# Low parts of the first projection's weights on VectorE, with the opening and the first feed-forward groups reordered

## The chip, the cores and the metric

The kernel runs on one core of one Trainium2 chip. The metric is the device time of one execution in microseconds; a kernel's time is the median of its runs. Five engines matter: TensorE (PE in the profile; its weight loads are PEld), VectorE (DVE), ScalarE (ACT), GpSimd (POOL), and SyncE (SP), which issues most DMAs.

## The reference

One block of a bidirectional encoder, on 1024 tokens of width 1024, in float32:

```python
h = layer_norm(x)
proj = h @ w_in                       # 1024 x 11776: q, k, v of 24 attention heads; q, two forget gates,
                                      # input and output gate of 8 recurrent heads; two merge gates
att = dilated_attention(aq, ak, av)   # three groups of 8 heads, dilations 1, 4, 16, windows of 128, 512, 2048
rec = hgrn2(hq, hf_fwd, hf_bwd, hi, hg, lower_bounds)   # chunkwise gated recurrence, both directions
merged = sigmoid(ga) * (att @ w_att_up) + sigmoid(gh) * (rec @ w_hgrn_up)
h = layer_norm(ALPHA * h + merged @ w_o)
gate, up = split(h @ w_ffn_in)        # 1024 x 5632
h = layer_norm(ALPHA * h + (silu(gate) * up) @ w_ffn_out)
```

## The kernel before

**Products in three passes.** Every float32 operand of a large product is split into a high part, `w_hi`, a cast to the rounded format that TensorE multiplies fast, and a low part, `w_lo = w - w_hi`. A product is `hi*hi + hi*lo + lo*hi`, three matmuls (`mm3`, L301 to L303), the third of which needs the low part of the weight:

```python
nc.tensor.matmul(ps, whi, xhi, start=first, stop=False, **kw)   # L301
nc.tensor.matmul(ps, whi, xlo, start=False, stop=False, **kw)   # L302
nc.tensor.matmul(ps, wlo, xhi, start=False, stop=last, **kw)    # L303
```

**Seven products for eight.** Each matrix product over 1024 x 256 of the weights and all tokens is done by a scheme of Strassen's kind: weights and activations are cut into 2 x 2 blocks, sums of blocks are made (`s1` to `s4` of the weights, `t1` to `t4` of the activations), and seven products of blocks, numbered 1, 2, 5, 6, 3, 7, 4 by `PRODUCTS`, take the place of eight. One product is twelve matmuls of 128 x 512 (four steps over the contraction, three passes), and its weight block, 128 x 4 x 128, is what the profile shows as 128x512. `wkeep` holds a partial result that was copied or added out of a PSUM bank; the last add goes into `evh`.

**The stream of the first projection (L556 to L658).** `stream` runs over groups of weight tiles, two groups (`g` = 0, 1) in turn. For each product `i` of the sequence it issues the sums of product `i + 5` (two on VectorE, L574 and L576 or L579, one on GpSimd, L575), then `prep(i + 3)`, then the twelve matmuls of product `i`, then its evacuation. `prep` makes the cast on ScalarE (`cast`, L585) and the low part (`rest`, L590) on GpSimd. Tiles `w_hi` and `w_lo` have four buffers each, so that weights are ready at most three products ahead. `evac_ahead` gives casts, lows and evacuations a higher priority than other work in the program's order.

**What runs between the products.** `phase1` puts pieces of other work between the steps of the stream: for the attention heads far and near units (`att_far`, `att_near`; the near unit scales its probabilities at L1159), and for each recurrent head `hgrn_side` with scans (L1263), reciprocals (L1274, L1277), products with them (L1278, L1279), and the chain of states `hR` (L1319, L1320), all on VectorE. At the end of the stream `load_split` (L1404) fetches the attention's output back and splits it, its low part (`att_lo`) on GpSimd, by L280.

**The opening (L661).** For the first two groups the order of work is written out by hand: the layer norm of the eight token blocks (`R.stats`, `R.norm`), transposes (`R.turn`), copies out of PSUM (`R.copy`), sums (`R.sum`), high and low parts of the activations (`R.hi`, L426, and `R.lo`, L432), and the first fourteen products, some in halves of 256 columns. Here the low parts of weights are on VectorE but for seven on GpSimd.

**The feed-forward opening (L1585 to L1627, and L1760 on).** `Group` does the same scheme for the feed-forward weights. The order around its first two groups, `g0` and `g1`, is again written out (`in_order`): `prep` makes a block's sum (L100), cast and low part (L276, L280), `late_block` fetches and splits one block of the activations as they arrive (`xb22`, `xt3`, `xt4`; four casts and four lows on VectorE), and `out` evacuates: a sum, a tanh on ScalarE (L1703) and a multiply on VectorE (L1704).

Each engine works through its own list of instructions; semaphores carry waits between engines. Weights come through DMAs that SyncE issues.

Of the kernel before, what the change touches and what calls it, by code (L numbers as in the profile page):

```python
# [81 lines left out]
class Group:  # L82
# [43 lines left out]
            o.nc.scalar.copy(t, ps)  # L126
        return t

    def out(self, i, l, ps, add):
        with self.o.tc.high_priority(offset=self.o.evac_ahead):  # L130
            self.evac(i, l, ps, add)

    def first(self):
        self.m1 = self.keep(self.product(1, 1, True))
# [15 lines left out]
class Block:  # L150
# [193 lines left out]
    def rows_in(self, pool):  # L344
# [14 lines left out]
        class Rows:  # L359
# [24 lines left out]
            @staticmethod  # L384
            def copy(t, q, on):
                g, b = self.col["gin"], self.col["bin"]
                if t < 4:
                    v = V[t, q] = self.half3("v11") if q == 0 else (
                        self.half3("v21") if t == 0 else pool.tile([128, 4, 128], F32, name=f"v21{t}"))
                else:  # L390
                    if q == 0:
# [164 lines left out]
    def stream(self, tiles):  # L556
# [37 lines left out]
        def prep(i):  # L594
            if i >= len(seq):
                return
            with tc.high_priority(offset=self.evac_ahead):
                cast(i)
                rest(i, nc.gpsimd)

        def bank(n, g, b):
            return self.ps_pj(2 * g + (n + b) % 2)
# [58 lines left out]
    def opening(self, pool, A, at, first, cast, rest, sums, product, evacuate):  # L661
# [63 lines left out]
        R.hi("b11", 2)  # L725
        R.hi("b21", 2)
        R.lo("b11", 2)
        R.turn(4, 0, 1)
        weight(2, 0, gps)
        R.copy(3, 0, "act")  # L730
        R.copy(3, 1, "dve")
        R.lo("b21", 2)
        R.norm(5)
        R.hi("b11", 3)
        R.hi("b21", 3)
        R.stats(6)
        R.lo("b11", 3)
        R.lo("b21", 3)
        weight(2, 1, gps)
        product(at[0, 2], 0)  # L740
        product(at[0, 1], 1)
        product(at[1, 1], 1)
# [4 lines left out]
        R.sum("t1", 4)  # L747
        R.hi("t1", 4)
        R.copy(4, 1, "act")
        R.lo("t1", 4)  # L750
# [5 lines left out]
        R.stats(7)  # L756
        R.copy(5, 0, "act")
        R.turn(6, 0, 1)
        sums(at[0, 6], dve)
        R.lo("t2", 4)  # L760
        evacuate(at[1, 1])
        R.sum("t1", 5)
        R.hi("t1", 5)
        R.copy(5, 1, "act")
        R.lo("t1", 5)
        cast(at[0, 6])
        R.sum("t2", 5)
        R.hi("t2", 5)
        R.norm(7)
        rest(at[0, 6], dve)  # L770
        R.copy(6, 0, "dve")
        sums(at[1, 6], dve)
        R.lo("t2", 5)
        cast(at[1, 6])
        evacuate(at[0, 2], later)
        cast(at[0, 5])
        product(at[0, 6], 0)
        R.turn(7, 0, 1)
        R.copy(6, 1, "act")
        evacuate(at[1, 2], later)  # L780
        R.sum("t1", 6)
        R.hi("t1", 6)
        rest(at[1, 6], dve)
        rest(at[0, 5], dve)
        R.copy(7, 0, "act")
        cast(at[1, 5])
        R.sum("t2", 6)
        R.hi("t2", 6)
        R.lo("t1", 6)
        rest(at[1, 5], dve)  # L790
        product(at[1, 6], 0)
        product(at[0, 5], 0)
        product(at[1, 5], 0)
        R.copy(7, 1, "act")
        R.sum("t1", 7)
        R.hi("t1", 7)
        R.lo("t2", 6)
        R.sum("t2", 7)
        R.hi("t2", 7)
        R.lo("t1", 7)  # L800
# [17 lines left out]
        evacuate(at[1, 6])  # L818
        R.sum("t3", 4)
        R.sum("t3", 5)  # L820
        R.hi("t3", 4, 5)
        evacuate(at[0, 5])
        R.sum("t3", 6)
        R.sum("t3", 7)
        evacuate(at[1, 5])
        R.lo("t3", 4, 5)
        R.hi("t3", 6, 7)
        R.lo("t3", 6, 7)
# [572 lines left out]
    def pool(self, name, side="left"):  # L1401
        return self.tc.tile_pool(name=name, bufs=1, side=side, reuse_waits="tile")

    def load_split(self, pool, src, hi, lo):  # L1404
        raw = pool.tile([128, T], F32, name="st_raw", tag="st", bufs=4)
        self.nc.sync.dma_start(raw, src)
        self.split(hi, lo, raw)

    def phase1(self):

# [17 lines left out]
        for k in work:  # L1428
# [16 lines left out]
            elif not units and not now:  # L1445
# [26 lines left out]
    def phase2(self):  # L1472
        nc = self.nc
        gc, bc = self.col["g1"], self.col["b1"]
        with ExitStack() as es:
# [208 lines left out]
    def ffn_in(self):  # L1684

        nc = self.nc
        with ExitStack() as es:
# [7 lines left out]
            def evac_of(f):  # L1695
                C[f] = c = fp.tile([128, T], F32, name="fc", tag="fc", bufs=4)
                th = fp.tile([128, T], F32, name="fth", tag="fth", bufs=2)

                def evac(i, l, ps, add):
                    s = slice(HALF * l, HALF * (l + 1))  # L1700
                    if i == 0:
                        nc.vector.tensor_add(c[:, s], add, ps)
                        nc.scalar.activation(th[:, s], c[:, s], AF.Tanh, scale=0.5)  # L1703
                        nc.vector.scalar_tensor_tensor(th[:, s], th[:, s], 1.0, c[:, s], op0=OP.add, op1=OP.mult)  # L1704
                        return
                    u = ps
                    if add is not None:
# [51 lines left out]
            for g, e in zip(self.ahead, self.first_evac):  # L1759
                g.evac = e  # L1760
            with self.in_order():
                g0.out(0, 0, g0.c11, g0.m1)
                g0.m5 = g0.keep(g0.product(5, 2, True))
                g1.prep(5)
                g0.u2 = g0.keep(g0.product(6, 1, False))
                g1.out(0, 0, g1.c11, g1.m1)
                g1.prep(6)
                splits = late_block(0)
                g0.prep(3)
                g1.m5 = g1.keep(g1.product(5, 2, True))  # L1770
# [7 lines left out]
                g0.out(0, 1, g0.product(3, 2, False), g0.u2)  # L1778
                g1.prep(3)
                splits = late_block(2)  # L1780
                g0.out(1, 1, g0.product(7, 1, False), g0.m5)
                g1.prep(7)
                g1.out(0, 1, g1.product(3, 2, False), g1.u2)
                g0.prep(4)
                for f in splits:
                    f()
                nxt = self.ffn_raws(FS[2])
                g1.out(1, 1, g1.product(7, 1, False), g1.m5)
                g0.out(1, 0, g0.product(4, 1, False), None)
            combine(0, 0)  # L1790
            held = (g1.out(1, 0, g1.product(4, 1, False), None) for _ in range(1))
# [350 lines left out]
```

## Time and profile before

| what | value |
| --- | --- |
| time, median of 3 runs (lowest, highest) | 2131.01 us (2128.5, 2132.04) |
| the profiled execution: its time, its span | 2132.19 us, 2130.4 us |
| mean granted TensorE clock | 0.984 |
| TensorE busy | 2040.0 us, 96% |
| VectorE busy | 1380.2 us, 65% |
| GpSimd busy | 1178.6 us, 55% |
| ScalarE busy | 918.1 us, 43% |

The span runs from the first to the last instruction. In a list of groups a row has line, engine, operation, tiles, shapes and count, then busy time in us, the mean of one in ns, and the idle time ahead of them with what ended it. A row of a timeline has start and length in us and, in brackets, the idle time just before with its releaser. A row of waits reads: who waited, for whom, total us, times, longest. A row of windows has the window, its length, the busy time of each engine asked for (PE, PEld, DVE, ACT, POOL in this order where all are shown), the granted clock, the DMA share and GB/s.

### The profile page before, as it was taken

The numbers are of one execution on the slowest core, as the hardware profiler recorded it, in microseconds if no ns is written. First come the engines' busy times: TensorE is split into PE (matmuls) and PEld (weight loads), VectorE is DVE, ScalarE is ACT, GpSimd is POOL, SyncE is SP. The second block draws the span as 40 slices with busy tenths as digits, with TensorE's granted clock in tenths as the row PEclk, the third lists the DMA queues.
The fourth block names the chain that finished last, engine by engine and source line by source line (L and its number), as shares of the span: only waits on it lengthen the run. The fifth ranks groups of instructions, "written<-read, shape, count | busy, mean of one in ns | idle before, by whom it ended". The sixth has DMA issues, their size and how long they took to land.

```text
span 2130.4 us, 31395 instructions
## 1 busy us (share of the span) xinstructions
PE 2040.0 (96%) x11037; PEld 1687.0 (79%) x11037; DVE 1380.2 (65%) x2176; ACT 918.1 (43%) x1871; POOL 1178.6 (55%) x943
## 2 busy tenths in 40 slices
PE   5899999999999999989999999999899999999998
PEld 5778887878878888778888788887688888888886
DVE  7857646876468754778535812347768778677965
ACT  6544454444544445544355432144444444444330
POOL 2366653566435764466644864342566777665553
PEclk9999999999999999999999999999999999999999
DMA  5443442435323453333433865333544544449685
GB/s 202 129 124 126 140 130 85 144 119 161 120 94 131 144 164 116 109 123 119 153 126 129 270 210 159 99 124 107 186 137 154 174 156 163 146 155 332 199 260 171
DMA packets 296448, 324.21 MB, mean 152 GB/s; under 512 B 15905, under 2 KB 212834, under 8 KB 296290
## 3 DMA queue, kind: packets, MB, share of 16 engines
q1 hardware_dynamic: 290272, 302.05, 44.1%
q10 hardware_dynamic: 6018, 20.16, 2.4%
q8 instruction: 87, 1.43, 0.3%
q14 instruction: 71, 0.58, 0.1%
HBM read 211.78 MB, written 110.36 MB: 151 GB/s over the span
## 4 chain that ended last, share of the span: by engine, by line
PE 61%; DVE 6%; issue 4%; POOL 4%; DMA 2%; ACT 1%; SPq 0%; DVEq 0%; POOLq 0%; ACTq 0%
PE pj L301 13%; PE pj L303 12%; PE pj L302 12%; PE sd L303 6%; PE sd L301 6%; PE sd L302 6%; POOL w_lo L590 2%; PE sd L1359 1%; ACT p L1137 1%; DMA wa<-in_w_in_dram 1%; DVE hR L1320 1%; PE sd L1173 1%; DVE p L1159 1%; POOL w_lo L280 1%; DVE hR L1319 0%
## 5 line engine op out<-in xcount | busy, mean ns | idle before, releaser
L590 POOL TENSOR_TENSOR w_lo<-wa,w_hi 128x512 fp32r<-128x512 f32 x268 | 376.3, 1413 | 256.5 <-ACT w_hi L585 248.3
L585 ACT CAST w_hi<-wa 128x512 fp32r<-128x512 f32 x276 | 169.8, 617 | 216.6 <-PE pj L302 149.8
L280 POOL TENSOR_TENSOR w_lo<-f_raw,w_hi 128x512 fp32r<-128x512 f32 x110 | 176.4, 1614 | 112.0 <-ACT w_hi L276 51.9
L303 PE MATMUL pj<-xb22hi,w_lo 128*128 128x512 f32 x268 | 107.2, 400 | 7.2 <-POOL w_lo L590 6.3
L301 PE MATMUL pj<-xb22hi,w_hi 128*128 128x512 f32 x268 | 107.8, 402 | 3.7 <-ACT wkeep L606 3.7
L301 PE MATMUL pj<-xt1hi,w_hi 128*128 128x512 f32 (+1 forms) x276 | 108.0, 391 | 3.2 <-DVE evh L475 2.1
L302 PE MATMUL pj<-xb22lo,w_hi 128*128 128x512 f32 x268 | 107.0, 399 | 0.7 <-DVE xb22lo L280 0.7
L303 PE MATMUL pj<-xt1hi,w_lo 128*128 128x512 f32 (+1 forms) x276 | 106.6, 386 | 0.7 <-POOL w_lo L280 0.7
L302 PE MATMUL pj<-xt1lo,w_hi 128*128 128x512 f32 (+1 forms) x276 | 106.7, 387 | 0.0
L276 ACT CAST w_hi<-f_raw 128x512 fp32r<-128x512 f32 x110 | 67.8, 619 | 82.7 <-DVE f_raw L100 29.2
L575 POOL TENSOR_TENSOR wa<-wa,wa 128x512 f32<-128x512 f32 x44 | 62.0, 1410 | 72.2 <-DVE ws L574 58.7
L280 POOL TENSOR_TENSOR w_lo<-Wb,w_hi 128x512 fp32r<-128x512 f32 x47 | 64.5, 1374 | 58.2 <-ACT w_hi L276 56.7
L590 POOL TENSOR_TENSOR w_lo<-ws,w_hi 128x512 fp32r<-128x512 f32 x44 | 61.6, 1404 | 59.8 <-ACT w_hi L585 57.7
L301 PE MATMUL pj<-xb11hi,w_hi 128*128 128x512 f32 (+1 forms) x196 | 78.9, 403 | 6.4 <-DVE wkeep L507 4.0
L606 ACT COPY wkeep<-pj 128x512 f32<-128x512 f32 x138 | 80.2, 582 | 11.4 <-DVE evh L475 5.9
L301 PE MATMUL pj<-xt2hi,w_hi 128*128 128x512 f32 (+1 forms) x196 | 77.8, 397 | 5.3 <-ACT xt2hi L426 3.7
L574 DVE TENSOR_TENSOR ws<-wa,wa 128x512 f32<-128x512 f32 x46 | 39.5, 861 | 65.9 <-DMA wa<-in_w_in_dram 49.7
L303 PE MATMUL pj<-xt2hi,w_lo 128*128 128x512 f32 (+1 forms) x196 | 76.7, 391 | 5.5 <-POOL w_lo L590 5.3
L280 POOL TENSOR_TENSOR w_lo<-wsum,w_hi 128x512 fp32r<-128x512 f32 x44 | 66.0, 1499 | 28.1 <-ACT w_hi L276 27.5
L302 PE MATMUL pj<-xt2lo,w_hi 128*128 128x512 f32 (+1 forms) x196 | 76.8, 392 | 3.7 <-DVE xt2lo L432 3.7
L1311 ACT ACTIVATE hS<-hR,dec 128x128 f32<-128x128 f32 x112 | 44.5, 402 | 82.4 <-DVE hR L1320 59.1
L303 PE MATMUL pj<-xb11hi,w_lo 128*128 128x512 f32 (+1 forms) x196 | 77.7, 397 | 0.6 <-POOL w_lo L590 0.6
(431 smaller groups left out, 6620.5 us busy)
## 6 DMA issues: line engine op xcount, KB each, us to landing
wa<-in_w_in_dram SPq DMA_DIRECT2D x184, 256.0 KB, 3.1
f_raw<-in_w_ffn_in_dram SPq DMA_DIRECT2D x44, 512.0 KB, 4.2
Wb<-in_w_ffn_out_dram SPq DMA_DIRECT2D x40, 256.0 KB, 5.1
tg<-evh SPq DMA_DIRECT2D x32, 256.0 KB, 3.4
tg<-tg SPq DMA_DIRECT2D x16, 512.0 KB, 3.4
y<-ahs SPq DMA_DIRECT2D x16, 512.0 KB, 3.4
ah<-xt SPq DMA_DIRECT2D x8, 512.0 KB, 6.1
rec<-hg ACTq DMA_DIRECT2D x8, 512.0 KB, 3.5
```

Source lines behind the costliest of these rows:

```text
L276: nc.scalar.copy(hi, src)
L280: e.tensor_sub(lo, src, hi.bitcast(F32))
L301: nc.tensor.matmul(ps, whi, xhi, start=first, stop=False, **kw)
L302: nc.tensor.matmul(ps, whi, xlo, start=False, stop=False, **kw)
L303: nc.tensor.matmul(ps, wlo, xhi, start=False, stop=last, **kw)
L574: nc.vector.tensor_add(a["s1"], a["a21"], a["a22"])
L575: third.tensor_sub(a["a21"], a["a11"], a["a21"])
L585: nc.scalar.copy(ready[i][0], A[g][self.PRODUCTS[p][0]])
L590: e.tensor_sub(lo, A[g][self.PRODUCTS[p][0]], hi.bitcast(F32))
L606: nc.scalar.copy(t, ps)
L1137: nc.scalar.activation(z, z, AF.Exp, bias=N0[p, hd, tt:tt + 1], scale=QSCALE, accum_out=L0[p, hd, tt:tt + 1])
L1311: nc.scalar.activation(S[:, c, :], E, AF.Copy, scale=dec[:, 1, c:c + 1])
```

## The change

Four parts:

1. `prep` in `stream` calls `rest(i, nc.vector)`: the lows of the first projection's weights go from GpSimd to VectorE. In the instruction lists GpSimd has 5 of them in place of 312, VectorE 317 in place of 10.
2. `load_split` takes `parts`: the four low parts of the attention's output are made in two halves each, on VectorE.
3. In the opening some steps are put in another order, and two weights' lows go from GpSimd to VectorE.
4. In the feed-forward opening `g0.prep(5)` stands before the last turn and `g1.prep(5)` before the rest of it; the sums `s3` are named early, products are in another order, the splits of the late blocks come after the next weights' sums, and the multiply after the tanh (`bend`) is issued later than its tanh.

Three places show how the engines' lists change. The first is VectorE at the first recurrent head: `w_lo` is a low part of weights, `fa` and `fb` are the forget gates of the two directions, `qd` takes the reciprocals. Before:

```order
L579 TENSOR_TENSOR wa_943<-wa_943,wa_806 128x512
L1263 SCALAR_TENSOR_TENSOR fa<-fa,d_1123 128x512
L1274 RECIPROCAL qd<-fa 128x4x64 x2
L1263 SCALAR_TENSOR_TENSOR fa<-fa,d_1123 128x512
L1263 SCALAR_TENSOR_TENSOR fb<-fb,d_1126 128x528 x2
L507 TENSOR_TENSOR wkeep<-wkeep,pj 128x512
L1274 RECIPROCAL qd<-fa 128x4x64 x2
L1277 RECIPROCAL qd<-fb 128x4x64 x4
L486 TENSOR_TENSOR evh<-wkeep,pj 128x512
```

After:

```order
L590 TENSOR_TENSOR w_lo<-wa_765,w_hi 128x512
L1265 SCALAR_TENSOR_TENSOR fa<-fa,d_1123 128x512
L1265 SCALAR_TENSOR_TENSOR fb<-fb,d_1126 128x528
L1276 RECIPROCAL qd<-fa 128x4x64 x2
L1265 SCALAR_TENSOR_TENSOR fa<-fa,d_1123 128x512
L1279 RECIPROCAL qd<-fb 128x4x64 x2
L1265 SCALAR_TENSOR_TENSOR fb<-fb,d_1126 128x528
L590 TENSOR_TENSOR w_lo<-wa_815,w_hi 128x512
L507 TENSOR_TENSOR wkeep<-wkeep,pj 128x512
L590 TENSOR_TENSOR w_lo<-ws_1137,w_hi 128x512
L1276 RECIPROCAL qd<-fa 128x4x64 x2
```

The lows of two neighbouring products (`wa_765`, `wa_815`) now have four scans and four reciprocals between them, and the next low stands behind `wkeep`. (Line numbers behind the opening are shifted by the change: L1263 before is L1265 after, L1274 is L1276, L1277 is L1279.)

The second place is ScalarE in the opening, where a wait of TensorE ends: `wkeep` is a copy that frees a bank, `xt3hi` the high part of an operand. Before:

```order
L585 CAST w_hi<-wa_368 128x512
L606 COPY wkeep<-pj 128x512
L426 CAST xt3hi<-vt 128x4x128 x2
L606 COPY wkeep<-pj 128x512 x2
L426 CAST xt3hi<-vt 128x4x128 x2
```

After:

```order
L585 CAST w_hi<-wa_368 128x512
L606 COPY wkeep<-pj 128x512 x2
L426 CAST xt3hi<-vt 128x4x128 x2
L606 COPY wkeep<-pj 128x512
L426 CAST xt3hi<-vt 128x4x128 x2
```

One of the two copies behind the first pair of casts has moved ahead of it.

The third is VectorE in the feed-forward opening: `f_raw<-f_raw,wsum` is a sum of weights, `xb22lo` and `xt3lo` are low parts of late blocks of the activations, `fc` and `fth` an evacuation and its multiply (L1702 and L1704 before are L1709 and L1713 after). Before:

```order
L100 TENSOR_TENSOR f_raw<-f_raw,wsum 128x512
L280 TENSOR_TENSOR xb22lo<-t_raw,xb22hi 128x512 x4
L280 TENSOR_TENSOR xt3lo<-t_raw,xt3hi 128x512 x4
L1702 TENSOR_TENSOR fc<-wkeep,pj 128x512
L1704 SCALAR_TENSOR_TENSOR fth<-fth,fc 128x512
L100 TENSOR_TENSOR f_raw<-f_raw,wsum 128x512
```

After:

```order
L100 TENSOR_TENSOR f_raw<-f_raw,wsum 128x512
L1713 SCALAR_TENSOR_TENSOR fth<-fth,fc 128x512
L280 TENSOR_TENSOR xb22lo<-t_raw,xb22hi 128x512 x4
L1709 TENSOR_TENSOR fc<-wkeep,pj 128x512
L100 TENSOR_TENSOR f_raw<-f_raw,wsum 128x512
L1713 SCALAR_TENSOR_TENSOR fth<-fth,fc 128x512
L1709 TENSOR_TENSOR fc<-wkeep,pj 128x512
L280 TENSOR_TENSOR xt3lo<-t_raw,xt3hi 128x512 x4
```

The second sum has moved from behind both sets of four lows to between them.

The diff, cut to its core:

```diff
@@ -596,7 +596,7 @@
             with tc.high_priority(offset=self.evac_ahead):
                 cast(i)
-                rest(i, nc.gpsimd)
+                rest(i, nc.vector)
...
@@ -725,18 +725,20 @@
         R.lo("b11", 2)
+        R.norm(5)
         R.turn(4, 0, 1)
-        weight(2, 0, gps)
+        cast(at[0, 2])
         R.copy(3, 0, "act")
         R.copy(3, 1, "dve")
         R.lo("b21", 2)
-        R.norm(5)
+        rest(at[0, 2], dve)
...
         R.lo("b11", 3)
+        cast(at[1, 2])
         R.lo("b21", 3)
-        weight(2, 1, gps)
+        rest(at[1, 2], dve)
         product(at[0, 2], 0)
...
@@ -818,11 +820,11 @@
         evacuate(at[1, 6])
         R.sum("t3", 4)
         R.sum("t3", 5)
+        evacuate(at[0, 5])
         R.hi("t3", 4, 5)
-        evacuate(at[0, 5])
+        evacuate(at[1, 5])
         R.sum("t3", 6)
         R.sum("t3", 7)
-        evacuate(at[1, 5])
         R.lo("t3", 4, 5)
...
-    def load_split(self, pool, src, hi, lo):
+    def load_split(self, pool, src, hi, lo, parts=()):
         raw = pool.tile([128, T], F32, name="st_raw", tag="st", bufs=4)
         self.nc.sync.dma_start(raw, src)
-        self.split(hi, lo, raw)
+        if not parts:
+            self.split(hi, lo, raw)
+        for s in parts:
+            self.split(hi[:, s], lo[:, s], raw[:, s], eng_lo="dve")
...
-                    self.load_split(self.sp, self.att_d[i], self.ah[:, i, :], self.al[:, i, :])
+                    self.load_split(self.sp, self.att_d[i], self.ah[:, i, :], self.al[:, i, :],
+                                    [slice(0, HALF), slice(HALF, T)])
...
                 g0.first()
+                g0.prep(5)
                 second, last = turn(7)
-                g0.prep(5)
+                g0.prep(6)
                 second()
                 g1.first()
-                g0.prep(6)
+                g1.prep(5)
                 rest()
                 last()
...
             with self.in_order():
-                g0.out(0, 0, g0.c11, g0.m1)
+                bends = []
                 g0.m5 = g0.keep(g0.product(5, 2, True))
-                g1.prep(5)
-                g0.u2 = g0.keep(g0.product(6, 1, False))
-                g1.out(0, 0, g1.c11, g1.m1)
                 g1.prep(6)
                 splits = late_block(0)
+                g0.out(0, 0, g0.c11, g0.m1, bends)
+                g0.u2 = g0.keep(g0.product(6, 1, False))
                 g0.prep(3)
+                bends.pop()()
                 g1.m5 = g1.keep(g1.product(5, 2, True))
-                splits += late_block(1)
-                for f in splits[:4]:
+                for f in splits:
                     f()
+                splits = late_block(1)
+                g1.out(0, 0, g1.c11, g1.m1, bends)
+                g1.prep(3)
                 g1.u2 = g1.keep(g1.product(6, 1, False))
+                g0.sum("s3")
+                bends.pop()()
+                g0.out(0, 1, g0.product(3, 2, False), g0.u2, bends)
+                for f in splits:
+                    f()
                 g0.prep(7)
-                for f in splits[4:]:
+                splits = late_block(2)
+                g1.sum("s3")
+                bends.pop()()
+                g1.out(0, 1, g1.product(3, 2, False), g1.u2, bends)
...
```

More of the change, by code (lines that the diff above doesn't have):

```diff
@@ L127, in keep, with out @@
         return t
-    def out(self, i, l, ps, add):
+    def out(self, i, l, ps, add, later=None):
         with self.o.tc.high_priority(offset=self.o.evac_ahead):
-            self.evac(i, l, ps, add)
+            self.evac(i, l, ps, add, later)
     def first(self):
@@ L390, in copy @@
                 else:
-                    if q == 0:
+                    if (t, 0) not in V:
                         V[t, 0], V[t, 1] = hold("vt")[1]
@@ L749, in opening @@
         R.copy(4, 1, "act")
+        R.stats(7)
         R.lo("t1", 4)
@@ L755, in opening @@
         R.hi("t2", 4)
-        R.stats(7)
         R.copy(5, 0, "act")
         R.turn(6, 0, 1)
-        sums(at[0, 6], dve)
+        R.norm(7)
         R.lo("t2", 4)
@@ L764, in opening @@
         R.copy(5, 1, "act")
+        sums(at[0, 6], dve)
+        R.turn(7, 0, 1)
         R.lo("t1", 5)
@@ L768, in opening @@
         R.hi("t2", 5)
-        R.norm(7)
         rest(at[0, 6], dve)
+        R.copy(6, 1, "act")
+        R.lo("t2", 5)
         R.copy(6, 0, "dve")
[L772 to L780, printed above, removed]
         R.sum("t1", 6)
         R.hi("t1", 6)
[L783 to L786, printed above, removed]
+        product(at[0, 6], 0)
+        sums(at[1, 6], dve)
+        cast(at[1, 6])
         R.sum("t2", 6)
@@ L789, in opening @@
         R.lo("t1", 6)
+        evacuate(at[0, 2], later)
+        cast(at[0, 5])
+        R.copy(7, 0, "act")
+        R.lo("t2", 6)
+        evacuate(at[1, 2], later)
+        rest(at[1, 6], dve)
+        rest(at[0, 5], dve)
+        cast(at[1, 5])
+        R.copy(7, 1, "act")
+        R.sum("t1", 7)
+        R.hi("t1", 7)
         rest(at[1, 5], dve)
@@ L793, in opening @@
         product(at[1, 5], 0)
[L794 to L797, printed above, removed]
         R.sum("t2", 7)
@@ L1697, in evac_of, with evac @@
                 th = fp.tile([128, T], F32, name="fth", tag="fth", bufs=2)
-                def evac(i, l, ps, add):
+                def evac(i, l, ps, add, later=None):
                     s = slice(HALF * l, HALF * (l + 1))
@@ L1703, in evac, with bend @@
                         nc.scalar.activation(th[:, s], c[:, s], AF.Tanh, scale=0.5)
-                        nc.vector.scalar_tensor_tensor(th[:, s], th[:, s], 1.0, c[:, s], op0=OP.add, op1=OP.mult)
+                        def bend():
+                            nc.vector.scalar_tensor_tensor(th[:, s], th[:, s], 1.0, c[:, s], op0=OP.add, op1=OP.mult)
+                        if later is None:
+                            bend()
+                        else:
+                            later.append(bend)
                         return
@@ L1761, in ffn_in @@
             with self.in_order():
-                g0.out(0, 0, g0.c11, g0.m1)
+                bends = []
                 g0.m5 = g0.keep(g0.product(5, 2, True))
-                g1.prep(5)
-                g0.u2 = g0.keep(g0.product(6, 1, False))
-                g1.out(0, 0, g1.c11, g1.m1)
                 g1.prep(6)
                 splits = late_block(0)
+                g0.out(0, 0, g0.c11, g0.m1, bends)
+                g0.u2 = g0.keep(g0.product(6, 1, False))
                 g0.prep(3)
+                bends.pop()()
                 g1.m5 = g1.keep(g1.product(5, 2, True))
-                splits += late_block(1)
-                for f in splits[:4]:
-                    f()
+                for f in splits:
+                    f()
+                splits = late_block(1)
+                g1.out(0, 0, g1.c11, g1.m1, bends)
+                g1.prep(3)
                 g1.u2 = g1.keep(g1.product(6, 1, False))
-                g0.prep(7)
-                for f in splits[4:]:
-                    f()
-                g0.out(0, 1, g0.product(3, 2, False), g0.u2)
-                g1.prep(3)
-                splits = late_block(2)
+                g0.sum("s3")
[3 more added lines that the diff above has]
+                    f()
+                g0.prep(7)
+                splits = late_block(2)
+                g1.sum("s3")
+                bends.pop()()
+                g1.out(0, 1, g1.product(3, 2, False), g1.u2, bends)
+                g1.prep(7)
+                for f in splits[:2]:
+                    f()
+                bends.pop()()
                 g0.out(1, 1, g0.product(7, 1, False), g0.m5)
-                g1.prep(7)
-                g1.out(0, 1, g1.product(3, 2, False), g1.u2)
                 g0.prep(4)
-                for f in splits:
+                for f in splits[2:]:
                     f()
@@ L1788, in ffn_in @@
                 g1.out(1, 1, g1.product(7, 1, False), g1.m5)
+                g1.prep(4)
                 g0.out(1, 0, g0.product(4, 1, False), None)
```

## The prediction

> **What bounds the kernel now.** I read the page's span and busy times first, then who waits for whom, then single stretches.
>
> ```profile
> span 2130.4 us, 31395 instructions
> PE 2040.0 (96%) x11037; PEld 1687.0 (79%) x11037; DVE 1380.2 (65%) x2176; ACT 918.1 (43%) x1871; POOL 1178.6 (55%) x943
> ```
>
> TensorE sets the time: it is busy 2040.0 of 2130.4 us, so all that a change to other engines can win is about 90 us of idle TensorE, plus what idling costs in clock. The change adds and removes no matmul. The idle time has these owners (waits of TensorE, then of VectorE):
>
> ```profile
> PE pj L303 <- POOL w_lo L590: 12.4, 11, 2.7
> PE sd L1173 <- DVE p L1159: 8.4, 6, 2.7
> PE pj L301 <- DVE evh L475: 5.4, 5, 2.8
> PE sd L1336 <- DVE hR L1319: 4.8, 2, 4.2
> PE pj L301 <- DVE wkeep L507: 4.0, 1, 4.0
> ...
> DVE ws L574 <- DMA wa<-in_w_in_dram: 49.7, 21, 6.5
> ```
>
> A short stall can cost twice. The columns here are window, TensorE busy, granted clock, DMA:
>
> ```profile
> 459.50:463.00 3.50, 3.50 (x10) 0.51 0.23 80
> 1193.40:1200.20 6.80, 6.09 (x14) 0.50 0.93 315
> ...
> 458.40 0.47 PE L301 MATMUL pj<-xb11hi,w_hi 128*128 128x512 f32 x1 [3.96 <-DVE wkeep L507]
> 1194.11 0.79 PE L303 MATMUL pj<-xb22hi,w_lo 128*128 128x512 f32 x1 [2.62 <-POOL w_lo L590]
> 116.09 0.50 PE L303 MATMUL pj<-xb22hi,w_lo 128*128 128x512 f32 x1 [2.73 <-POOL w_lo L590]
> ...
> 116.00:123.00 7.00, 6.91 (x30) 5.74 (x31) 6.62 (x15) 4.39 (x10) 2.00 (x3) 1.00 0.60 189
> ```
>
> After the stall of 3.96 us the clock was 0.51 for 3.5 us: some 1.7 us of work lost. After the one of 2.62 it was 0.50 for 6.8 us: 3.4 lost. After the one of 2.73 at 116 us it stayed 1.00 (the column before the last two). So a stall of two to four us costs nothing, 1.7 or 3.4 us on top; I price it at 1.7.
>
> The Trainium skill ("TensorE: Matmul & The Clock Gate", Part 1: The HAM clock gate) has half rate follow at least one idle window of about 3.4 us. The 2.62 us stall above was shorter and was followed by half rate, so the trace disagrees; by the page none of the 3.4 us at 1194 would be had back by ending that stall, and the sum below would stand 3.4 higher.
>
> **The change part by part.** The main part moves the low parts of the first projection's weights.
>
> ```profile
> L590 POOL TENSOR_TENSOR w_lo<-wa,w_hi 128x512 fp32r<-128x512 f32 x268 | 376.3, 1413 | 256.5 <-ACT w_hi L585 248.3
> L590 POOL TENSOR_TENSOR w_lo<-ws,w_hi 128x512 fp32r<-128x512 f32 x44 | 61.6, 1404 | 59.8 <-ACT w_hi L585 57.7
> ...
> 50.15 0.68 DVE L590 TENSOR_TENSOR w_lo<-wa,w_hi 128x512 fp32r<-128x512 f32 x1
> 100.00:1225.00 1125.00, 1082.69 (x6768) 898.54 (x6768) 726.88 (x1345) 519.51 (x1176) 646.13 (x561) 0.98 0.42 134
> 450.00:500.00 50.00, 46.05 (x224) 38.42 (x223) 42.24 (x50) 19.50 (x39) 30.50 (x28) 0.97 0.36 116
> ```
>
> Of 312 on GpSimd at 1.41 us, 307 go to VectorE, where the opening's own ones take 0.68 us. GpSimd loses about 430 us, VectorE gains 307 x 0.68 = 209. VectorE (third group of numbers in a window's row) would then be busy (727 + 209) / 1125 = 83% of the projection stage, and in 450 to 500 us 42.2 + 14 x 0.68 = 51.8 of 50: full. What gives time back is that its instructions with two inputs in SBUF now run long beside GpSimd:
>
> ```profile
> L576 DVE TENSOR_TENSOR wa<-ws,wa 128x512 f32<-128x512 f32 x46 | 50.0, 1091 | 18.6 <-POOL w_lo L590 16.0 <-POOL wa L575 2.6
> 47.14 0.69 DVE L576 TENSOR_TENSOR wa<-ws,wa 128x512 f32<-128x512 f32 x1
> L1159 DVE TENSOR_SCALAR p<-p,W 64x128 f32<-64x128 f32 x16 | 15.2, 952 | 0.4
> L1159 DVE TENSOR_SCALAR p<-p,W 128x256 f32<-128x256 f32 x56 | 15.1, 342 | 0.0
> ```
>
> L576 takes 1.09 us on average in the whole run, 0.69 in the opening; L1159 takes 952 ns on 64x128 and 342 on a tile four times as large. That is 46 x 0.40 = 18 us for L576 and 16 x 0.61 = 10 for L1159.
>
> (1) *Waits on GpSimd's lows*: 12.4 us, 11 times, plus 3.4 us of clock at 1194. There a low of the attention's output stands ahead in GpSimd's queue, and the change makes those four on VectorE in halves (3.47 us each in the first row below, against about four half-size ones of the kind of 0.68 us, so some 1.4):
>
> ```profile
> 1188.38 3.47 POOL L280 TENSOR_TENSOR att_lo<-st_raw,att_hi 128x1024 fp32r<-128x1024 f32 x1
> ...
> 103.76 0.50 PE L303 MATMUL pj<-xt2hi,w_lo 128*128 128x512 f32 x1 [1.47 <-POOL w_lo L590]
> ```
>
> Head 0's two waits (1.47 and 2.73) come back under (6). Left are 8.2 + 3.4 = 11.6; I take **-11**, between -16 and 0.
>
> (2) *Near attention*: TensorE waits 8.4 us for L1159. Four units lose 2.4 us each of contention there, 9.8 in all; the ends are -12 (the wait and two times 1.7 of clock) and 0 (another step of the softmax takes over). I take **-9**, since the rows of L1159 run back to back on VectorE:
>
> ```profile
> 355.71 7.57 DVE L1159 TENSOR_SCALAR p<-p,W 64x128 f32<-64x128 f32 x18
> 358.14 0.44 PE L1173 MATMUL sd<-tabs_sb,p 128*128 128x128 f32 x2 [2.30 <-DVE p L1159]
> ```
>
> (3) *Waits on VectorE's sums and states* (L475, L507, L1319): 14.2 us, with three or four losses of clock some 20. They are later by the lows now ahead of them, earlier by the 18 us of L576 and as much of its like. Ends +7 and -20; I take **-6**.
>
> (4) *Opening*. The copies that free the banks stand behind a pair of casts:
>
> ```profile
> 65.99 1.22 ACT L426 CAST xt3hi<-vt 128x512 fp32r<-128x512 f32 x2 [0.88 <-DVE vt L417]
> 67.12 1.07 ACT L606 COPY wkeep<-pj 128x512 f32<-128x512 f32 x2
> 67.75 0.79 PE L301 MATMUL pj<-xb22hi,w_hi 128*128 128x512 f32 x1 [3.65 <-ACT wkeep L606]
> ```
>
> The change puts one copy ahead of the casts. Without the 0.88 and 1.22 us it ends 2 us sooner, and the wait of 3.65 may fall below what loses clock. The casts come 0.5 later, and VectorE's lows of that operand are the next thing that is late. The earlier moves of the opening (a norm ahead of a turn, casts apart from their lows) shift halves of products that still end behind the same low, so I cost them at nothing; if that cover fails, about 1 us. **-3**, between -5.4 and +1.
>
> (5) *Feed-forward opening*. A sum that a cast waits for stands behind eight lows of the stage's input:
>
> ```profile
> 1499.81 5.21 DVE L280 TENSOR_TENSOR xb22lo<-t_raw,xb22hi 128x512 fp32r<-128x512 f32 x4 [2.03 <-ACT xb22hi L276]
> 1504.95 2.49 DVE L280 TENSOR_TENSOR xt3lo<-t_raw,xt3hi 128x512 fp32r<-128x512 f32 x4
> 1510.12 0.62 ACT L276 CAST w_hi<-f_raw 128x512 fp32r<-128x512 f32 x1 [1.42 <-DVE f_raw L100]
> 1510.79 0.73 PE L301 MATMUL sd<-xb22hi,w_hi 128*128 128x512 f32 x1 [2.25 <-ACT w_hi L276]
> 1494.73 0.50 PE L301 MATMUL sd<-xt1hi,w_hi 128*128 128x512 f32 x1 [1.89 <-ACT w_hi L276]
> ```
>
> That sum now stands between the two sets of four lows, 2.5 us of work earlier; the sum behind the wait of 1.89 us is issued before the rest of the last turn; the multiplies after the tanh (L1704) no longer hold up either. 2.25 + 1.89 and one or two losses of clock make 7.5 at most. The lows of the input are then later, each ahead of its own product: **-5**, between -7.5 and +2.
>
> (6) *The lows behind VectorE's bursts.* VectorE's rows in the trace come in the order of the program. At head 0 the order before the second group's low (`w_lo<-wa_815`) now has two scans on `fa`, two on `fb`, two reciprocals on `fa` and two on `fb`:
>
> ```profile
> 94.92 1.22 DVE L1263 TENSOR_TENSOR_SCAN fa<-fa,d 128x512 f32<-128x512 f32 x1
> 96.17 3.36 DVE L1274 RECIPROCAL qd<-fa 128x256 f32<-128x256 f32 x2
> 100.52 4.29 DVE L1263 TENSOR_TENSOR_SCAN fb<-fb,d 128x528 f32<-128x528 f32 x2
> 108.59 6.53 DVE L1277 RECIPROCAL qd<-fb 128x256 f32<-128x256 f32 x4
> ```
>
> 2 x 1.22 + 4.29 + 3.36 + 6.53 / 2 = 13.4 us. The cover is three prepared products: the 30 matmuls of 116 to 123 us took 6.91, so 0.23 each, twelve make a product of some 2.7 us, three 8.2. So 5.2 us of stall and 1.7 of clock, 6.9. The order has five such bursts in eight heads: at most 5 x 6.9 = 34, at least 0 where TensorE has the head's own matmuls to run. Knowing no more, I take half: **+17**. VectorE's waits for weight DMAs (49.7 us, 21 times) now hold up lows as well; their mean of 2.4 us lies within the cover: 0, and 6.5 (the longest) if one meets a burst.
>
> Sum: -11 - 9 - 6 - 3 - 5 + 17 = **-17**. The profiled execution took 2132.2 us, 1.2 above the median of the runs: 2114.
>
> **The rivals.**
> *VectorE becomes the feeder (slower).* Each low that stands behind a burst comes after its product's turn: all five bursts cost 6.9 us (34), (3) turns to +2 because its sums are behind the lows too, and (1), (2) and (5) give 11 + 9 + 5. That is +11 without the opening: 2142. For it: 51.8 us of work in a 50 us window, and a low that is in no one's way on GpSimd. Against it: the cover of 8.2 us, and the time that L576 and its like give back. It decides where bursts cost more than 34 / 5 = 6.9 each, or the gains stay under 30.
> The Trainium skill ("TensorE: Matmul & The Clock Gate", Architectural detail) gives VectorE a strictly first-in first-out queue of eight, so that a low cannot pass a burst; the quoted run of scans and reciprocals, in program order, agrees.
>
> *The lows were not what was late (no change).*
>
> ```profile
>   ACT w_hi L585: 308.2, 143
> ```
>
> GpSimd stood idle 308.2 us before its lows until the cast was there. Where it is early, a faster low wins nothing: of (1), (2) and (3) half is left (13), (4) and (5) give 8, and the bursts take 17: -4, at 2127; with less, 2131.
>
> *The cover holds everywhere (faster still).* (6) is then 0 and the rest -34: 2097. Against it speaks that head 0's stall is already visible in the order.
>
> **How the numbers follow.** Forecast 2114, own range 2101 to 2126: 0.52. Faster still: 0.11. No change: 0.16. Slower: 0.21. A measurement tells a difference of about 0.2%, 4.3 us. Faster then has 0.52 + 0.11 and 0.02 from the third case, 0.65; same 0.14; slower 0.21. The range goes from 2096 to 2141.
>
> **What would show it.** (1) TensorE's waits for `w_lo` from GpSimd vanish, none longer than 1 us from 1185 to 1225. (2) L1159 on 64x128 falls to 0.3 to 0.4 us, L576 to 0.7 to 0.8. (4) no 3.65 us before the first block of `xb22`. (5) TensorE idles under 6 us from 1475 to 1540. (6) a wait for VectorE's `w_lo` L590 of 3 to 8 us near 100 us, and those waits sum to 10 to 25 us with five or so over 2. I am wrong if they exceed 35 us, or if VectorE's busy time in 100 to 1225 us does not lie between 850 and 940.

## The result, and the profile after

The changed kernel takes 2103.43 us (median of 4 runs, 2099.65 to 2104.6), the kernel before in the same company 2129.76 (2126.7 to 2132.04). The ratio is 0.9873, with a 95% interval of 0.9859 to 0.9887: 1.3% faster, 26 us where 17 were forecast. The profiled execution has a span of 2102.7 us, 27.7 less than the one before. The page's span and busy times, and the answer on the clock:

```profile
span 2102.7 us, 31221 instructions
PE 2025.0 (96%) x11037; PEld 1677.2 (80%) x11037; DVE 1477.4 (70%) x2491; ACT 921.9 (44%) x1875; POOL 749.7 (36%) x632
core 0: 2102.7 us, clock 0.992
```

TensorE has the same matmuls and is busy 15.0 us less; it is idle 77.7 us where it was idle 90.4. So in this pair of executions the 27.7 us are 12.7 of shorter waits and 15.0 of clock: the granted clock rose from 0.984 to 0.992. How the gain divides is not the same in each execution. The changed kernel's other three had a clock of 0.987 to 0.988 and took about as long (2099.65 to 2104.6 us); its four average 0.989, and 60 executions of the kernel before, timed beside the experiments, average 0.985 (0.981 to 0.990). By these means the clock is worth some 7 us of the 26, an estimate from TensorE's 2040 us. TensorE's waits now:

```profile
PE pj L303 <- DVE w_lo L590: 12.4, 9, 4.6
PE pj L301 <- DVE evh L486: 7.6, 4, 3.5
PE pj L301 <- DVE evh L475: 4.1, 3, 1.7
PE sd L1338 <- DVE hR L1321: 2.9, 3, 1.5
PE pj L301 <- DVE wkeep L507: 2.5, 1, 2.5
...
PE sd L1175 <- DVE p L924: 0.2, 1, 0.2
```

The waits for low parts amount to 12.4 us as before, but for VectorE's lows and in other places; the 8.4 us for the near unit's scaling are gone. VectorE's operations take less time than before (groups of VectorE by line and shape, after; L1161 and L1322 are L1159 and L1320 of before):

```profile
L590 DVE TENSOR_TENSOR w_lo<-wa,w_hi 128x512 fp32r<-128x512 f32 x271 | 199.0, 737 | 92.0 <-ACT w_hi L585 87.9 <-PE sd L966 2.0 <-DMA at2q<-evh 1.2
L576 DVE TENSOR_TENSOR wa<-ws,wa 128x512 f32<-128x512 f32 x46 | 36.5, 794 | 2.3 <-POOL wa L575 1.2
L579 DVE TENSOR_TENSOR wa<-wa,wa 128x512 f32<-128x512 f32 x46 | 32.3, 701 | 0.5
L1322 DVE TENSOR_SCALAR hR<-hR,dec 128x128 f32<-128x128 f32 x96 | 28.5, 297 | 1.7
L1161 DVE TENSOR_SCALAR p<-p,W 64x128 f32<-64x128 f32 x16 | 6.7, 418 | 0.4
...
100.00:1225.00 1125.00, 1096.14 (x6880) 911.94 (x6880) 825.79 (x1660) 535.73 (x1200) 233.34 (x261) 0.99 0.43 138
```

And two groups of before, beside the row of L576 that the prediction shows:

```profile
L579 DVE TENSOR_TENSOR wa<-wa,wa 128x512 f32<-128x512 f32 x46 | 48.8, 1067 | 24.8 <-POOL w_lo L590 24.6
L1320 DVE TENSOR_SCALAR hR<-hR,dec 128x128 f32<-128x128 f32 x96 | 49.4, 514 | 2.8
```

L576 falls from 1091 to 794 ns, L579 from 1067 to 701, the second step of the chain of states from 514 to 297. VectorE's busy time in 100 to 1225 us is 825.8 us. With the lows at 0.68 us and nothing else changed it would have been 727 + 209 = 936: some 110 us came back, of which the five groups L574 (861 to 686 ns), L576, L579, L1320 and L1159 make 67. The prediction had worked out 28 from rows and put down "as much of its like" beside the 18 of L576.

Where along the program the time went is seen from the start of the n-th low-part matmul (L303, counted from 0) in the profiled executions, in us after the kernel before. E1 and E2 are the two halves of the change, E3 an experiment below:

```
n-th L303   start before   changed   E1 lows only   E2 all but lows   E3 echo
180            160.7         +2.3        +2.4            +0.4           +5.8
420            399.2         -8.1        -7.5            -2.9          +12.2
720            693.5        -18.4       -15.6            -4.9          +25.3
1200          1150.3        -20.1       -18.9            -5.0          +55.5
1260          1202.6        -26.8       -23.3           -11.8          +51.3
1620          1454.8        -25.4       -22.1            -7.8          +57.9
1740          1558.5        -27.7       -16.7            -9.7          +55.6
last          2121.9        -27.4       -16.0           -10.1          +55.6
```

The opening and the first recurrent head lose 2 us, the stream gains 22 from there to 1150, its end another 7, the feed-forward opening 2. From 1740 on nothing differs. One execution stands behind each column, and some 5 us of a difference can be chance: E6 below, whose code is that of the kernel before up to the feed-forward opening, stands 4.8 us ahead at the 1200th. So the stream's 22 us are clear, and the smaller steps are not. (E1's profiled execution, with a span of 2114.5 us, was slower than the median of its runs.)

### The profile page after: what moved, and what is told of

The parts are those of the page before. It is cut to its first block, busy times and chain, and to the rows that moved or that the text cites. A ratio compares the mean times of both kernels' runs of the same rounds, so it can differ in the third digit from the quotient of the medians.

```text
span 2102.7 us, 31221 instructions
## 1 busy us (share of the span) xinstructions
PE 2025.0 (96%) x11037; PEld 1677.2 (80%) x11037; DVE 1477.4 (70%) x2491; ACT 921.9 (44%) x1875; POOL 749.7 (36%) x632
## 4 chain that ended last, share of the span: by engine, by line
PE 74%; DVE 11%; DMA 5%; issue 5%; ACT 3%; POOL 2%; SPq 0%; DVEq 0%; ACTq 0%; POOLq 0%
PE pj L301 16%; PE pj L303 16%; PE pj L302 16%; PE sd L301 6%; PE sd L303 6%; PE sd L302 6%; DVE w_lo L590 2%; PE sd L1361 2%; DVE qd L1276 1%; POOL w_lo L280 1%; DVE qd L1279 1%; PE sd L1123 1%; DMA a<-ah 1%; DMA wa<-in_w_in_dram 1%; DMA ghi<-gs3h 1%
## 5 line engine op out<-in xcount | busy, mean ns | idle before, releaser
L590 DVE TENSOR_TENSOR w_lo<-wa,w_hi 128x512 fp32r<-128x512 f32 x271 | 199.0, 737 | 92.0 <-ACT w_hi L585 87.9
L280 POOL TENSOR_TENSOR w_lo<-f_raw,w_hi 128x512 fp32r<-128x512 f32 x110 | 176.0, 1611 | 107.4 <-ACT w_hi L276 45.4
L303 PE MATMUL pj<-xt1hi,w_lo 128*128 128x512 f32 (+1 forms) x276 | 107.7, 390 | 0.7 <-POOL w_lo L280 0.5
L303 PE MATMUL pj<-xb22hi,w_lo 128*128 128x512 f32 x268 | 104.8, 393 | 1.4 <-POOL w_lo L280 0.9
L303 PE MATMUL pj<-xt2hi,w_lo 128*128 128x512 f32 (+1 forms) x196 | 77.9, 399 | 11.7 <-DVE w_lo L590 10.7
L301 PE MATMUL pj<-xt,w_hi 128*128 128x512 f32 x184 | 74.3, 405 | 5.2 <-DVE evh L486 3.5
L303 PE MATMUL pj<-xb11hi,w_lo 128*128 128x512 f32 (+1 forms) x196 | 77.4, 395 | 1.5 <-DVE w_lo L590 1.0
L302 PE MATMUL pj<-xb11lo,w_hi 128*128 128x512 f32 (+1 forms) x196 | 76.6, 391 | 0.0
L301 PE MATMUL pj<-xb21hi,w_hi 128*128 128x512 f32 (+1 forms) x196 | 76.4, 390 | 0.0
```

Source lines behind the costliest of these rows:

```text
L280: e.tensor_sub(lo, src, hi.bitcast(F32))
L590: e.tensor_sub(lo, A[g][self.PRODUCTS[p][0]], hi.bitcast(F32))
```

## The experiments

The theory: the stream gains because GpSimd no longer works beside VectorE, whose shorter operations end TensorE's waits and with them the half clock. The rivals: the lows simply come sooner; the reorderings and halves carry the gain; the bursts eat most of what the move wins. Times of the kernel before differ by call (2130.9 to 2131.9 us); each ratio is against the kernel before on the same chip.

**E1, the lows alone.** The kernel before with one line changed:

```diff
-                rest(i, nc.gpsimd)
+                rest(i, nc.vector)
```

> The kernel before with one line changed: the stream's lows on VectorE. The theory (the stream gains because GpSimd no longer runs beside VectorE and no low is late at a matmul) expects 2107 to 2113 us, 17 to 23 below before, most of it between 160 and 1150 us, and L576 near 0.75 us. The rival (the reorderings and the halves carry the gain, the move of the lows pays for its bursts only) expects 2122 us or more.

2109.62 us against 2131.34, ratio 0.9905 (0.9886 to 0.9924): 21.7 less. L576 took 797 ns. The rival in which the reorderings and halves carry the gain is out. Whether the lows gain by coming sooner or by leaving VectorE alone, this run can't tell; E3 bears on that.

**E2, all but the lows.** The changed kernel with that line put back.

> The changed kernel with the stream's lows back on GpSimd. The theory expects 2119 to 2125 us: the opening about 0, the halves of the attention's output about -5, the feed-forward opening about -3. The rival expects 2112 us or less.

2124.23 us, ratio 0.9969 (0.9954 to 0.9983): 7.1 less. The two halves add up to 28.8, close to the 26.3 of the whole; there is little between them that either needs of the other. (The three parts of this half, each alone in E5 to E7, add up to 2.7 less, not 7.1. Why they give more together was not tried.)

**E5, E6, E7, the rest in its parts**, each alone on the kernel before. E5 is the opening's new order:

> The kernel before with the opening's new order alone. The prediction's step (4) expects 3 us less, between -5.4 and +1; the profile of the changed kernel less its lows, which at 161 us stands where the kernel before stands, expects no difference, within 2 us.

2132.92 us against 2130.92, ratio 1.0017 (1.0008 to 1.0026): 2 us slower by the medians, 1.7 to 5.5 by the interval. TensorE's long wait between 60 and 80 us:

```profile
78.39 0.47 PE L301 MATMUL pj<-xt,w_hi 128*128 128x512 f32 x1 [3.62 <-DVE evh L486]
```

The wait of 3.65 us for `wkeep` at 67.75 is gone, as the order promised; one of 3.62 stands 11 us later. The changed kernel has the same wait, 3.54 us at 78.86. VectorE's list ahead of it, in the changed kernel, is full:

```profile
75.63 1.29 DVE L432 TENSOR_TENSOR xt<-v,xt 128x512 fp32r<-128x512 f32 x2
76.83 1.28 DVE L590 TENSOR_TENSOR w_lo<-wa,w_hi 128x512 fp32r<-128x512 f32 x2
78.03 0.68 DVE L486 TENSOR_TENSOR evh<-wkeep,pj 128x512 f32<-128x512 f32 x1
```

Against the kernel before, TensorE is ready for this product 6.9 us sooner in E5, but VectorE begins the evacuation that it waits for (L486) only 3.2 us sooner, at 77.56 us for 80.80. So the product itself starts 3.2 us earlier, and at the 180th low-part matmul the profiled execution is still 0.9 us ahead. Where the median loses its 2 us is not shown.

E6 is the feed-forward opening's new order:

> The kernel before with the feed-forward opening's new order alone. Step (5) expects 5 us less, between -7.5 and +2; the gain is in 1440 to 1530 us, where the stalls of 1.89 and 2.25 us go. The rival (the lows of the late blocks become what is late) expects less than 2 us.

2128.79 us, ratio 0.9993 (0.9981 to 1.0004): a gain cannot be told from none. In its profiled execution the waits of 1.89 and 2.25 us are gone, but others stand there: for casts and lows of the next products' weights, and one of 2.06 us for a sum of VectorE's (`fu`, an evacuation):

```profile
1488.57 0.50 PE L301 MATMUL pj<-xt2hi,w_hi 128*128 128x512 f32 x1 [1.15 <-ACT w_hi L276]
1490.24 0.50 PE L303 MATMUL pj<-xt2hi,w_lo 128*128 128x512 f32 x1 [0.94 <-POOL w_lo L280]
1506.98 0.50 PE L301 MATMUL pj<-xt3hi,w_hi 128*128 128x512 f32 x1 [1.44 <-ACT w_hi L276]
1512.96 0.47 PE L301 MATMUL sd<-xt4hi,w_hi 128*128 128x512 f32 x1 [2.06 <-DVE fu L1717]
```

E7 is the attention's output in halves on VectorE:

```diff
+        for s in parts:
+            self.split(hi[:, s], lo[:, s], raw[:, s], eng_lo="dve")
```

> The kernel before with the four low parts of the attention's output in halves on VectorE alone. The theory (they block GpSimd's queue ahead of the weights' lows) expects 3 to 7 us less, all of it between 1180 and 1225 us, where the waits for w_lo of 0.75, 2.62, 0.84 and 0.58 us and the half clock of 6.8 us vanish. If VectorE's sharing with GpSimd is what is late there, nothing changes, within 2 us.

2128.29 us, ratio 0.9988 (0.9978 to 0.9999): 2.6 less, just clear of nothing and under the 3 to 7 expected. The waits for `w_lo` between 1180 and 1225 us are all gone. In their stead two for VectorE's evacuations stand there, the longer one 2.74 us:

```profile
1200.22 0.47 PE L301 MATMUL pj<-xb11hi,w_hi 128*128 128x512 f32 x1 [2.74 <-DVE evh L486]
```

**E3, an echo on GpSimd.** In the changed kernel each low on VectorE gets a twin on GpSimd that nobody reads. It has the size, the trigger and two inputs like the old one, but both inputs are `w_hi`, and it writes bf16:

```diff
                 rest(i, nc.vector)
+                hi = ready[i][0]
+                z = self.ws.tile([128, 4, 128], mybir.dt.bfloat16, name="echo", tag="echo", bufs=1)
+                nc.gpsimd.tensor_sub(z, hi.bitcast(F32), hi.bitcast(F32))
```

> The changed kernel, and beside each low on VectorE GpSimd makes a subtraction of the same size from w_hi into a scratch tile in bf16 that nobody reads: GpSimd is as busy beside VectorE as before, but no matmul and no VectorE sum waits for it. If the gain is VectorE freed of GpSimd, it is lost for the larger part: 2118 us or more, VectorE busy over 900 us in 100 to 1225 us (826 without), L576 over 1.0 us. If the gain is that the lows come sooner, it stays: 2100 to 2107 us.

2189.81 us against 2131.34, ratio 1.0275 (1.0258 to 1.0293): 86 us above the changed kernel, 58 above the kernel before. Rows of GpSimd, VectorE, the window and TensorE's waits:

```profile
L602 POOL TENSOR_TENSOR echo<-w_hi 128x512 bf16<-128x512 f32 x305 | 396.9, 1301 | 401.6 <-ACT w_hi L585 394.4 <-DMA v<-at2v 1.2 <-DMA hg<-hg2g 0.2
...
L590 DVE TENSOR_TENSOR w_lo<-wa,w_hi 128x512 fp32r<-128x512 f32 x271 | 247.8, 918 | 72.7 <-ACT w_hi L585 66.5 <-PE sd L902 3.4 <-PE sd L969 1.8
L576 DVE TENSOR_TENSOR wa<-ws,wa 128x512 f32<-128x512 f32 x46 | 47.2, 1026 | 4.4 <-POOL wa L575 3.4
...
100.00:1225.00 1125.00, 1050.85 (x6557) 870.71 (x6556) 893.45 (x1596) 499.32 (x1138) 579.63 (x537) 0.97 0.37 120
...
PE sd L1341 <- DVE hR L1324: 23.3, 8, 5.4
PE pj L303 <- DVE w_lo L590: 23.2, 15, 3.1
```

VectorE's lows take 918 ns for 737, L576 is back at 1026; VectorE is busy 893 us in the window, a little under the 900 expected. The window holds fewer matmuls than in the changed kernel (6557 for 6880). Over the same ones, from the 180th to the 1200th low-part matmul, VectorE is busy 822 us for 715 and the stretch takes 1039 us for 967. The chain of states alone makes TensorE wait 23.3 us, where it had been 2.9. So VectorE can take the lows over only because GpSimd lays them down.

One part of the gain this leaves open. In the kernel before, VectorE's sums also stood behind GpSimd's lows, L576 for 16.0 us and L579 for 24.6. With the echo that doesn't come back (4.4 and 0.5 us ahead of them in all), so its loss is not of this kind; what the end of these waits is worth in the gain was not separated.

**E9 and E12, GpSimd at work without reading.** E9 fills each `w_lo` tile with zeros, twice, before VectorE writes into it:

```diff
+                for _ in range(2):
+                    nc.gpsimd.memset(ready[i][1].bitcast(F32), 0.0)
                 rest(i, nc.vector)
```

> The changed kernel, where GpSimd fills each w_lo tile twice with zeros (128x512, 0.53 us each in the kernel before's own) before VectorE writes the low part into it: GpSimd is busy 320 us more in the same stretch and at a like pace, but its instructions read nothing. If the echo's 86 us came of GpSimd reading beside VectorE, this costs little: 2101 to 2112 us, L576 under 0.85 us. If any GpSimd work beside VectorE slows it, 2140 us or more.

2126.6 us against 2130.97, ratio 0.9981 (0.9969 to 0.9994), between the two expectations. L576 took 813 ns, so fills hardly stretch it; but the experiment also made a new wait:

```profile
DVE w_lo L590 <- POOL w_lo L600: 93.1, 74, 3.2
```

VectorE's lows stood 93 us behind the fills and 36 behind the casts, where in the changed kernel they stood 92 behind the casts alone. So the 23 us that it lost against the changed kernel cannot be put down to the sharing. E12 takes that wait away: GpSimd copies one column of `w_hi`, as the trigger, and fills a scratch tile.

```diff
+                nc.gpsimd.tensor_copy(z[:, 0, 0:1], hi.bitcast(F32)[:, 0, 0:1])
+                for _ in range(2):
+                    nc.gpsimd.memset(z, 0.0)
```

> As the echo of a subtraction, at the same trigger (the cast w_hi), but GpSimd copies one column of w_hi and then fills the scratch tile twice: it is as often at work beside VectorE, reads next to nothing, and neither a matmul nor VectorE waits for it. If the echo's loss came of GpSimd reading while VectorE adds two tiles, 2102 to 2112 us, lows and L576 under 0.80 us on average. If any GpSimd work beside VectorE costs the same, 2150 us or more. Where VectorE's operations on one tile (L1161, the second of the hR steps) are slowed by the fills as they were when w_lo was filled, the time lies between, 2112 to 2130 us.

2112.71 us against 2131.89, ratio 0.9908 (0.9889 to 0.9927), at the border of the first range expected and the third. The same views as of the echo, and two groups of VectorE's operations on one tile:

```profile
L604 POOL MEMSET echo<- 128x512 bf16 x610 | 321.9, 528 | 32.9
L602 POOL CAST echo<-w_hi 128x1 bf16<-128x1 f32 x305 | 123.5, 405 | 285.7 <-ACT w_hi L585 278.0
...
L590 DVE TENSOR_TENSOR w_lo<-wa,w_hi 128x512 fp32r<-128x512 f32 x271 | 200.8, 744 | 91.2 <-ACT w_hi L585 87.6 <-PE sd L971 2.0 <-DMA at2q<-evh 1.3
L576 DVE TENSOR_TENSOR wa<-ws,wa 128x512 f32<-128x512 f32 x46 | 35.0, 762 | 3.5 <-POOL wa L575 2.4
L1327 DVE TENSOR_SCALAR hR<-hR,dec 128x128 f32<-128x128 f32 x96 | 34.3, 357 | 1.7
L1166 DVE TENSOR_SCALAR p<-p,W 64x128 f32<-64x128 f32 x16 | 10.5, 654 | 0.4
...
100.00:1225.00 1125.00, 1092.77 (x6855) 906.67 (x6855) 834.39 (x1659) 532.21 (x1195) 664.17 (x1169) 0.99 0.42 137
```

GpSimd is busier here than in the echo (664 us against 580 in the window), and the kernel loses 9 us against the changed one by the medians, not 86. VectorE's operations on two tiles keep their length (744 and 762 ns); its operations on one tile are longer (357 for 297 ns, 654 for 418). So some nine tenths of the echo's loss came with GpSimd's two-input subtraction and do not come with fills, and the lesser rest goes with the fills. Another way for the echo to cost time is that it holds `w_hi`, which the next casts need. That is not it: ScalarE's casts waited 22.1 us for the echo in E3 and 45.4 us for the copies and fills in E12.

The Trainium skill ("SBUF — State Buffer", Who interferes with whom) says that a VectorE instruction with two inputs in SBUF contends with a GpSimd instruction that reads SBUF, not with one that only writes, and that VectorE's two-port modes contend with GpSimd. The rows of E3 and E12 agree with the first: 918 and 1026 ns beside reads, 744 and 762 beside fills. The one-tile operations, longer beside fills (357 and 654 ns), would fit the second, but no view shows the mode that they ran in.

**E4, E8, E11, E10, a better kernel.** E4 puts the lows that are issued while a recurrent head's scans and reciprocals are issued back on GpSimd:

```diff
-                rest(i, nc.vector)
+                rest(i, nc.gpsimd if getattr(self, 'burst', False) else nc.vector)
```

> The changed kernel with the lows that are issued while a recurrent head's scans and reciprocals are issued back on GpSimd (29 of 317). If the bursts are what the lows still wait for, the stalls of 2.7 us at 105 and 4.6 at 890 us go with their half clock: 2093 to 2099 us. If GpSimd's lows beside the scans cost as much as they save: 2101 to 2108 us.

2101.39 us, ratio 0.9864 (0.9846 to 0.9882), against 0.9873 (0.9859 to 0.9887) of the changed kernel: the same within the measurement. By the trace 24 of VectorE's 317 lows went back. TensorE's waits for VectorE's lows fell from 12.4 to 7.0 us, a gain in the profile that the time hardly shows. The wait of 4.63 us near 890 shrank to 0.94, but the one of 2.68 at head 0 stayed at 2.29.

E8 also moves the third of the weights' sums, the last steady work of GpSimd in the stream, to VectorE; E11 does that alone, without E4's lows:

```diff
-        def sums(i, third=nc.gpsimd):
+        def sums(i, third=nc.vector):
```

> The kernel with the bursts' 29 lows on GpSimd, and the third sum of the weights (44 of 1.43 us on GpSimd) on VectorE too. If what counts is only how little GpSimd reads beside VectorE, 2092 to 2099 us. If VectorE is now near its fill (821 of 1125 us, and 30 us more), 2100 to 2110 us, with longer waits for w_lo.

> The changed kernel with the third sums on VectorE, and all lows of the stream on VectorE. If the third sums are what gained, 2096 to 2100 us; if the bursts' lows on GpSimd are what gained, 2101 to 2106 us.

Both take 2097.92 us (0.985, 0.9834 to 0.9866; 0.9853, 0.9835 to 0.987), so what gain there is goes with the sums: 5.5 us on the changed kernel by the medians, 4 to 5 by the ratios, whose intervals overlap at their ends. The bursts' lows add nothing that shows. In E11 VectorE has 44 sums more and is hardly busy longer:

```profile
L576 DVE TENSOR_TENSOR wa<-ws,wa 128x512 f32<-128x512 f32 x46 | 31.8, 694 | 0.6
100.00:1225.00 1125.00, 1101.39 (x6915) 914.86 (x6914) 827.74 (x1705) 538.10 (x1202) 177.50 (x220) 1.00 0.43 140
```

827.7 us against 825.8: the sums' 31 us (44 of 0.70) were paid back by the rest, as with L576, at 694 ns now, and the lows, at 696 for 737.

E10 is E8 with the opening in its old order:

> The kernel of 2098 us (29 lows of the bursts on GpSimd, the third sums on VectorE) with the opening in the order of the kernel before. If the opening's new order costs what it cost alone, 2094 to 2097 us; if it gains in this company, 2100 to 2104 us.

2092.56 us against 2130.97, ratio 0.9824 (0.9807 to 0.9841): the fastest kernel of this study, 1.8% under the kernel before, 11 us under the changed one and below both ranges expected. Against E8 it is 5.4 us in the medians, more than the 2 that the opening's order cost alone; the two intervals of their ratios overlap at their ends, so the size of that step is uncertain.

## Why the prediction was right or wrong

Forecast 2114 us with a range of 2096 to 2141; measured 2103. The side and the mechanism were right; two of the six terms (4, 5) were too good and one (6) too bad, and these errors in part cancel. Step by step:

- **(1) Waits on GpSimd's lows, -11.** They vanished, and from 1185 to 1225 us no wait is longer than 0.64 us. (The 3.4 us of clock at 1194 were 3.0: TensorE was busy for 6.09 of the 6.8 us at half clock.) The stretch from the 1200th to the 1260th low-part matmul became 6.7 us shorter. The halves alone gave 2.6, since VectorE's evacuations were next.
- **(2) Near attention, -9.** Right: L1161 on 64x128 takes 418 ns for 952, a little over the 0.3 to 0.4 us predicted, and of the 8.4 us of waiting for it none are left. Between the 360th and 420th such matmul the kernel gains 6.1 us, between the 600th and 660th 4.4.
- **(3) Waits on sums and states, -6.** By name they fell from 14.2 to 9.5 us. L486, where no wait had stood, now has 7.6, 3.5 of them in the opening.
- **(4) Opening, -3.** Wrong in sign: alone it costs 2 us, outside the step's own -5.4 to +1. The step priced the wait that goes, 3.65 us, and named VectorE's lows as next, but gave that no price; a wait of equal length came 11 us later. In the profiled execution 3.2 us are still gained there and 0.9 at the 180th low-part matmul, so where the gain turns into a loss stays open.
- **(5) Feed-forward opening, -5.** The waits named are gone, but alone it gives 2.1 us and an interval that reaches no change: too large. The sign that TensorE would idle under 6 us from 1475 to 1540 did not come: it idles 7.3 us in the changed kernel, where it was 10.9, and the longest wait, 2.04 us, is for a sum of VectorE's that the step had not named.
- **(6) The lows behind bursts, +17.** The mechanism is there, in two of the five places:

```profile
105.55 0.50 PE L303 MATMUL pj<-xt2hi,w_lo 128*128 128x512 f32 x1 [2.68 <-DVE w_lo L590]
890.55 0.80 PE L303 MATMUL pj<-xt2hi,w_lo 128*128 128x512 f32 x1 [4.63 <-DVE w_lo L590]
...
889.80:896.60 6.80, 6.05 (x14) 0.50 0.36 116
```

  All waits for VectorE's lows are 12.4 us, 2.45 of them in the opening. The two above are 7.3, and the half clock behind the one at 890 cost half of 6.05 us of work, 3.0: some 10 us, where +17 was taken. Head 0 stalled 2.7 us for the 5.2 worked out: its burst ended at 104.8 after 11.2 us, not 13.4, since the scans on `fb` were shorter too (1.26 and 1.19 us for 2.1). E4 took two fifths of these waits away and won next to nothing, so half of the worst case was too much for this term.

The step that was mis-sized most is none of the six but the line ahead of them: 28 us of VectorE's time given back, some 46 with the "as much of its like" of (3), where 110 came. VectorE's busy time in the stream (826 us) fell outside the bounds that the prediction set itself (850 to 940), on the good side; by the prediction's own words that was a sign of being wrong, and it was, about the size. The window of 450 to 500 us, forecast full (51.8 us of 50), holds 43.5 us of VectorE's work. The prediction named the mechanism, instructions with two inputs in SBUF, but worked out two groups only: L576 and L1159 gave 22 us for its 28, while L574, L579 and the one-tile step of the chain of states, which it did not list, gave 45. The clock was the other: the prediction priced it per stall, and in the sum it is 15 of the 27.7 us in the profiled pair, some 7 by the means of all executions. The rival in which VectorE becomes the feeder is what E3 shows: it comes true when GpSimd's reads go on.

## What to carry to other kernels

Before work is moved off an engine that is not the bound, compare the mean of an operation beside that engine with its length alone, for all groups: here VectorE took on 209 us of work and its busy time rose by 99, and it took on a further 31 and rose by 2. Before a stall in a hand-written order is removed, price the engine that is late next at the same place: the opening and the feed-forward opening gave less here than their stalls promised. Some short stalls are paid twice through the clock, so the list of waits shows only a part of what can be won; how large a part differs from one execution to the next.

## What the runs showed of the hardware

Reads of GpSimd cost VectorE far more than its mere work: with 305 subtractions of 1.30 us beside it the kernel is 86 us slower, with 610 fills of 0.53 us and 305 one-column copies only 9. A one-column copy on GpSimd took 405 ns here, three quarters of a fill of 128x512.

The clock fell to half after stalls shorter than its own steps: the half clock lasts 3.41 us or a multiple of it, and after 2.32 us at 117.67 the next piece ran at 0.50, after 2.68 us at 105.55 it did not.

```profile
117.67 0.50 PE L301 MATMUL pj<-xt1hi,w_hi 128*128 128x512 f32 x1 [2.32 <-DVE evh L486]
101.28:104.69 3.41, 1.59 (x15) 1.00 0.00 0
104.69:108.11 3.42, 2.56 (x11) 1.00 0.27 77
114.94:118.35 3.41, 1.09 (x7) 1.00 0.29 82
118.35:121.76 3.41, 3.41 (x10) 0.50 0.51 169
```

The traces show what decides between the two (columns: window, length, TensorE busy, granted clock, DMA). In each trace the changes of clock lie on one grid of 3.41 us. The stall of 2.32 us falls into one step of the grid, in which TensorE idles 2.32 us; the longer one of 2.68 us is cut in two, 1.82 us in one step and 0.86 in the next. Over the 14 traces of this case there are 135 steps at full clock that are followed by half, each with at least 1.60 us of idle TensorE, and 8173 that are followed by full clock, none with more than 2.00 (up to 2110 us, from 30 us on, with ends of matmuls as the trace has them). So here a stall costs clock when about half a step is idle, and where the grid cuts it matters as much as its length. The two stalls on which the prediction set its price of 1.7 us differ in this way as well: in the kernel before, 1.95 us of one step were idle ahead of 1194 us, and 1.58 and 1.26 us of two steps ahead of 116.
